# Unused bf16 products ahead of TensorE's steps in the last four experts of a mixture-of-experts layer

## The chip, the core and the metric

The kernel runs on one core of a Trainium2 chip. The metric is device time in microseconds (us) of one execution. A core has engines that run side by side, each in its own order: TensorE (PE in the profile, with PEld for its weight loads), VectorE (DVE), ScalarE (ACT), GpSimd (POOL) and SyncE (SP), which here issues the transfers from HBM.

## The reference, cut to what matters

One layer of a decoder: a token mixer of two attentions, a norm, and then a mixture of experts over 256 tokens of width 1024 in fp32. A router picks 4 of 32 experts for each token. For each expert, on the rows `xb` that go to it:

```
gu = xb @ w_gu[e] + b_gu[e]                 # 1024 -> 2048
gate = minimum(gu[:, :1024], 7); up = clip(gu[:, 1024:], -7, 7)
act = (up + 1) * gate * sigmoid(1.702 * gate)
y[token] += weight * (act @ w_down[e] + b_down[e])   # 1024 -> 1024
```

The result is the norm of `alpha * h + y`. The weights of all 32 experts, six pieces of 2 MB an expert, are read from HBM once.

## The kernel before, in words

The mixer takes the first part of the span. Then a loop over `j` from 0 to 31 (line 1142) takes the experts one after the other, in an order that `SCHED` fixes by their rank in number of tokens; it gives each a block of 64 rows (two blocks for two of them) or, for those with few tokens, of 32 rows. The numbers of experts here are places in this order. Expert 27 has 64 rows and experts 28 to 31 have 32 each.

The weights of an expert come in six transfers, called chunks here: chunks 0 to 3 are `w_gu` and chunks 4 and 5 are `w_down`, of 2 MB each. They land in a ring of ten slots, in the order of the list `SEQUENCE`; `fill` (line 434) issues the next one on SP's queue when a slot comes free. In the last expert chunks 4 and 5 are issued as four halves of 1 MB, in the order (4, first), (5, first), (4, second), (5, second).

TensorE's work is cut into steps. `expert_in` (line 877) makes one half of `gu` from two chunks; `expert_out` (line 935) makes `dn` from chunks 4 and 5. With 32 rows a step multiplies two pieces of the contraction by 512 columns into four strips of the array, so that there are two steps to a chunk; with 64 rows there are four steps to a chunk. An fp32 product is two instructions in the trace, so that a chunk is 16 instructions. For the last expert `expert_out` works on 256 columns at a time: first all four steps of the left half, then all four of the right half.

`step` (line 164) runs a step and then what is due after it: `later(n, f)` puts f behind the n-th step from there. In this way the transposes of `gu` (tile `gup`, line 910, through the matrix of sums where there are 32 rows), the turning of the gates (`ogp`, line 840), the gathering of rows (`xgp`, line 855), the last norm's rows spread over the partitions (`lnp`, line 816) and the addition of `dn` to the sum (`y`, line 960) stand between the steps. `gup`, `ogp`, `xgp` and `lnp` share one PSUM tag, `tp`, with two buffers.

For `j` the loop does the first half of `gu` (`way_in(j, 0)`), `way_out(j - 1)`, and the second half of `gu`; for `j` = 31 both halves stand ahead of `way_out(30)`. Behind the loop stands a branch for experts that have more tokens than rows (line 1164; its body isn't run here), then `way_out(31)`, the norm and the output.

At its very start the kernel multiplies the bf16 tile `ones`, 128x128, by itself 31 times (tile `warm`, line 157). The result isn't used.

Of the kernel before, what the change touches and what calls it, by code (L numbers as in the profile page):

```python
# [7 lines left out]
F32 = mybir.dt.float32  # L8
# [11 lines left out]
NE = 32  # L20
# [47 lines left out]
def layer(ctx: ExitStack, tc: tile.TileContext, x_tok, x_t, wmix, b_gate, lam, subln, ln, lnc, w_r, b_r, *rest):  # L68
    nc = tc.nc
# [33 lines left out]
    ones = cp.tile([128, 128], BF)  # L103
# [15 lines left out]
    ps1 = ps1s.enter_context(tc.tile_pool(name="ps1", bufs=1, space=PSUM))  # L119
# [44 lines left out]
    def step(f):  # L164
        f()
        for d in waiting:
            d[0] -= 1
        due = [d for d in waiting if d[0] <= 0]
        waiting[:] = [d for d in waiting if d[0] > 0]
        for d in due:  # L170
            d[1]()
# [648 lines left out]
    def norm_spread():  # L820
        w = chunks["norm"]
        for i in range(4):
            later(3 + 3 * i, lambda i=i: nc.scalar.copy(w[:, i * 512:i * 512 + 512], spread(1, i)))

    def onehot(rank, oh):
        for t in range(2):
            nc.vector.tensor_scalar(oh[:, t], cst[:, C_IO:C_IO + oh.shape[2]], rank[t], None, op0=OP.is_equal)
# [19 lines left out]
    def gather(oh, n):  # L847
        xgs.append(xgs.pop(0))
        xg = xgs[-1][0].tile([128, 8, 128], F32, tag=xgs[-1][1], name="xg")

        def half(k):
            p = ps1.tile([128, 4, 128], F32, tag="tp", name="xgp", bufs=2)
            for i in range(4):
                for t in range(2):
                    nc.tensor.matmul(p[:, i, 0:n], x1[:, t, (k + i) * 128:(k + i) * 128 + 128], oh[:, t, 0:n],  # L855
                                     start=t == 0, stop=t == 1)
            assert len(rows_done) in (0, 4)
            if rows_done:
                nc.vector.tensor_copy(xg[:, k:k + 4, 0:n], p[:, :, 0:n])  # L859
                return  # L860

            for i in range(4):
                g, b = lncol[:, 0, k + i:k + i + 1], lncol[:, 1, k + i:k + i + 1]
                if i % 2:
                    nc.scalar.activation(xg[:, k + i, 0:n], p[:, i, 0:n], AF.Identity, bias=b, scale=g)  # L865
                else:
                    nc.vector.tensor_scalar(xg[:, k + i, 0:n], p[:, i, 0:n], g, b, op0=OP.mult, op1=OP.add)
        later(1, lambda: half(0))
        later(2, lambda: half(4))
        return xg  # L870

    def bias_of(w):
        bias = cp.tile([128, 16], F32, tag="bgu", name="bgu", bufs=3)
        nc.gpsimd.tensor_copy(bias, w[:, 4096:SLOT])  # L874
        return bias

    def expert_in(ws_, xg, at_, w, n, done, between=None):


        g = ps1.tile([128, 512], F32, tag="s", name="gu", bufs=2)  # L880
        m = 64 // w

        def some(k):
            for i in range(2 * m):
                e, u = divmod(i, 2)
                o = ((k + e) % 4 * 2 + u) * 512
                nc.tensor.matmul(g[i * w:i * w + w, :], xg[:, k + e, at_:at_ + w], ws_(2 * n + k // 4)[:, o:o + 512],  # L887
                                 start=k == 0, stop=k + m == 8)
        for k in range(0, 8, m):
            step(lambda: some(k))  # L890
            if done and (k + m) % 4 == 0:
                done(2 * n + k // 4)
            if between and 0 < k < 5:
                between(k + 3)
        return g
# [25 lines left out]
    def back(d, ogT, cs, ended=None, delay=2):  # L921

        dn = wk.tile([128, 512], F32, tag="gt", name="ds_", bufs=3)
        nc.scalar.copy(dn[:, cs], d)  # L924

        def add():
            for t in range(2):
                for n in range(2):
                    rs = slice(n * 64, n * 64 + 64)
                    add_to_y(ogT[rs, t], dn[rs, cs], t, n, cs)  # L930
                if ended:
                    ended(t, cs)
        later(delay, add)

    def expert_out(ws_, act, ogT, w, done, last=False):


        m = 64 // w

        def some(d, k, cs):  # L940
            q = slice(cs.start // 256, cs.stop // 256)
            for i in range(2 * m):
                n, e = divmod(i, m)
                of = ws_(4 + (k + e) // 4).rearrange("p (q k n c) -> p k n q c", q=2, k=4, n=2)
                nc.tensor.matmul(d[i * w:i * w + w, :].rearrange("p (q c) -> p q c", c=256), act[:, k + e],  # L945
                                 of[:, (k + e) % 4, n, q], start=k == 0, stop=k + m == 8, skip_group_check=True)

        for cs in [slice(0, 256), slice(256, 512)] if last else [slice(0, 512)]:
            d = ps1.tile([128, cs.stop - cs.start], F32, tag="s", name="dn", bufs=2)
            for k in range(0, 8, m):  # L950
                step(lambda: some(d, k, cs))
                if done and cs.stop == 512 and (k + m) % 4 == 0:
                    done(4 + k // 4)
            back(d, ogT, cs, last_norm if last else None, 0 if cs.start else 2)
# [8 lines left out]
    def cols(a, k, j):  # L963
        return [a[:, k + t, j:j + 1] for t in range(2)]

    def rank(j, b):

        if b == 0:
            return cols(rgs, 0, j)
        r = cp.tile([128, 2], F32, tag="rk", name="rk", bufs=4)  # L970
        nc.vector.tensor_scalar(r, rgs[:, 0:2, j], 64.0 * b, None, op0=OP.subtract)
        return [r[:, t:t + 1] for t in range(2)]
# [60 lines left out]
    def scale_rows():  # L1033

        def part(c, i):
            rows_done.append((c, i))
            p = spread(0, 2 * i + c)
            for t in range(2):
                z = x1[:, t, c * 512:c * 512 + 512]
                nc.vector.tensor_tensor(z, z, p, op=(OP.mult, OP.add)[i])  # L1040
        for c in range(2):
            for i in range(2):
                later(4 + 4 * c + 2 * i, lambda c=c, i=i: part(c, i))
# [32 lines left out]
    def prepare(j):  # L1076

        for b in range(len(SCHED[j][1])):
            if (j, b) not in place:
                oh = wk0.tile([128, 2, 128], F32, tag="oh", name="oh")  # L1080
                n, found = 0, {}
                for jb in blocks[blocks.index((j, b)):]:
                    w = SCHED[jb[0]][1][jb[1]]
                    if n + w > 128:
                        break
                    onehot(rank(*jb), oh[:, :, n:n + w])
                    found[jb] = n
                    n += w
                xg = gather(oh, n)
                place.update({jb: (xg, k) for jb, k in found.items()})  # L1090

    def residual(n):

        bdn = wk.tile([NE, 512], F32, tag="gt", name="bdn", bufs=3)
        nc.scalar.dma_start(bdn, b_down[:, n * 512:n * 512 + 512])
        aid = wk0.tile([128, 128], F32, tag="oh", name="aid")
        nc.vector.tensor_scalar(aid, ident, ALPHA, None, op0=OP.mult)
        for t in range(2):
            later(2 + t, lambda t=t: add_to_y(aid, x1[:, t, n * 512:n * 512 + 512], t, n))
        for t in range(2):  # L1100
            later(6 + t, lambda t=t: add_to_y(rgT[:, 2 + t], bdn, t, n))
# [16 lines left out]
    def done(j, c):  # L1118
        consumed.add((j, c))
        while order_left and order_left[0] in consumed:  # L1120
            order_left.pop(0)
            fill()
# [13 lines left out]
    def way_out(j):  # L1136
        ns = SCHED[j][1]
        for b, w in enumerate(ns):
            expert_out(lambda c: chunks[j, c], acts[j][b], ogTs[j][b], w,
                       (lambda c: done(j, c)) if b == len(ns) - 1 else None, j == NE - 1)  # L1140

    for j, (_, ns) in enumerate(SCHED):
        if j in RESIDUAL:
            residual(RESIDUAL.index(j))
        if j == NE - 3:
            norm_spread()
        if j + 1 < NE:
            prepare(j + 1)
        if j == RESIDUAL[0] - 1:
            scale_rows()  # L1150
        way_in(j, 0)
        if j == NE - 1:
            way_in(j, 1)
        if j:
            way_out(j - 1)
        ogTs[j] = [weighted(rank(j, b), cols(rgs, 2, j), w) for b, w in enumerate(ns)]
        if j < NE - 1:
            way_in(j, 1)
# [50 lines left out]
    for t, c in ((0, 1), (1, 0), (1, 1)):  # L1209
# [3 lines left out]
        for u in range(1 + t * c):  # L1213
            n = 512 >> t * c
# [112 lines left out]
```

## Time and profile before

| | us |
|---|---|
| median of 3 runs | 1212.2 |
| the three runs | 1212.0, 1212.2, 1214.49 |
| the profiled execution's own time | 1211.38 |
| its span, first to last instruction | 1209.6 |
| TensorE busy in the span | 1112.9 |
| mean granted TensorE clock | 0.958 of full speed |

The span is what the trace shows. The profiled execution's own time is 1.8 us longer than its span, and 0.8 us less than the median of the runs. Times below count from the start of the span.

### The profile page before, as it was taken

The page shows a single profiled execution, that of the slowest core. Times are in us where ns is not written, and L with a number is a line of the kernel's source. Part 1 is how long each engine was busy: PE and PEld are TensorE (multiplying, and loading weights), DVE is VectorE, ACT ScalarE, POOL GpSimd, SP SyncE. Part 2 cuts the span into 40 slices and gives each one's busy share as a digit, 9 for nine tenths or more (in the row PEclk, how much of TensorE's full clock was granted, in tenths as well). Part 3 has the DMA queues.
Part 4 walks back from the last instruction along what each step waited for, and adds up shares of the span by engine and source line. Part 5 has one row for each costly group of instructions (what it writes and reads, how often), then busy time and mean ns, then how long its engine had stood idle before and what let it go on. Part 6 is the DMA issues. An engine that isn't in the chain of part 4 may idle for free. (4 is left out here: it accounts for less than half of the span.)

```text
span 1209.6 us, 15833 instructions
## 1 busy us (share of the span) xinstructions
PE 1112.9 (92%) x6294; PEld 543.1 (45%) x6294; DVE 374.0 (31%) x974; ACT 264.7 (22%) x559; POOL 63.6 (5%) x142
## 2 busy tenths in 40 slices
PE   9999999999999999999999988988888887988765
PEld 7888768885443344343334423332323232322222
DVE  5677675675232212212211211221211121111103
ACT  5555564543111112111101110110010100001100
POOL 1233220001000000000000000000000000000001
PEclk9999999999999999999999998999989999978887
DMA  9574348577999999999999999999999999999994
GB/s 354 203 266 147 134 167 338 209 279 299 395 427 427 426 428 427 427 427 424 428 420 428 427 429 425 428 428 426 429 427 426 429 427 428 428 428 428 427 427 184
DMA packets 34350, 451.49 MB, mean 373 GB/s; under 512 B 4097, under 2 KB 5281, under 8 KB 6881
## 3 DMA queue, kind: packets, MB, share of 16 engines
q1 hardware_dynamic: 34176, 450.31, 89.4%
q8 instruction: 51, 0.84, 0.3%
q14 instruction: 27, 0.21, 0.0%
q10 hardware_dynamic: 96, 0.13, 0.0%
HBM read 449.37 MB, written 1.05 MB: 372 GB/s over the span
## 5 line engine op out<-in xcount | busy, mean ns | idle before, releaser
L887 PE MATMUL gu<-w,xg 128*64 128x512 f32 (+1 forms) x2176 | 420.2, 625 | 53.6 <-DMA w<-in_wg_dram 53.3
L887 PEld LDWEIGHTS gu<-w,xg 128*64 128x64 f32 (+1 forms) x2176 | 111.4, 127 | 280.3 <-issue 249.9
L945 PE MATMUL dn<-w,act 128*64 128x512 f32 (+2 forms) x1120 | 212.2, 621 | 24.8 <-DMA w<-in_wd_dram 23.8
L913 DVE TENSOR_TENSOR h<-gup,bgu 128x512 f32<-128x512 f32 (+1 forms) x68 | 39.6, 582 | 468.1 <-PE gup L908 256.6
L945 PEld LDWEIGHTS dn<-w,act 128*64 128x64 f32 (+1 forms) x1120 | 59.4, 129 | 149.8 <-issue 121.5
L152 DVE TENSOR_TENSOR wl<-w,wh 128x512 fp32r<-128x512 f32 x140 | 99.1, 730 | 61.1 <-ACT wh L151 60.4
L232 PE MATMUL acc<-wh,xh 128*128 128x512 f32 x256 | 105.0, 410 | 1.3 <-ACT wh L151 1.3
L233 PE MATMUL acc<-wl,xh 128*128 128x512 f32 x256 | 101.8, 398 | 1.4 <-POOL wl L152 0.8
L234 PE MATMUL acc<-wh,xl 128*128 128x512 f32 x256 | 101.1, 395 | 0.0
L151 ACT CAST wh<-w 128x512 fp32r<-128x512 f32 x148 | 89.0, 621 | 52.0 <-PE acc L234 39.9
L901 ACT COPY gt<-gu 128x512 f32<-128x512 f32 x68 | 39.9, 587 | 248.9 <-PE gu L887 248.7
L915 ACT ACTIVATE act<-h 128x256 f32<-128x256 f32 (+1 forms) x68 | 25.4, 374 | 256.0 <-DVE h L914 256.0
L855 PEld LDWEIGHTS xgp<-oh,x 128*128 128x128 f32 x448 | 56.4, 205 | 14.1 <-issue 12.1
L855 PE MATMUL xgp<-oh,x 128*128 128x128 f32 (+1 forms) x448 | 60.7, 293 | 0.6 <-ACT xg L865 0.6
L859 DVE COPY xg<-xgp 128x384 f32<-128x384 f32 (+1 forms) x18 | 11.1, 615 | 144.8 <-PE xgp L855 144.6
L232 PEld LDWEIGHTS acc<-wh,xh 128*128 128x128 f32 x256 | 49.8, 195 | 12.4 <-ACT wh L151 2.4
L233 PEld LDWEIGHTS acc<-wl,xh 128*128 128x128 f32 x256 | 49.7, 194 | 12.1 <-DVE wl L152 2.1
L234 PEld LDWEIGHTS acc<-wh,xl 128*128 128x128 f32 x256 | 49.6, 194 | 9.3
L874 POOL COPY bgu<-w 128x16 f32<-128x16 f32 x32 | 6.9, 215 | 856.9 <-DMA w<-in_wg_dram 768.1
L841 ACT COPY ogT<-ogp 128x256 f32<-128x256 f32 x34 | 12.7, 372 | 135.6 <-PE ogp L840 135.6
L910 PEld LDWEIGHTS gup<-cst,gt 128*128 128x128 f32 x224 | 29.5, 206 | 26.1 <-issue 24.4
L910 PE MATMUL gup<-cst,gt 128*128 128x64 f32 x224 | 33.5, 297 | 0.0
(333 smaller groups left out, 841.2 us busy)
## 6 DMA issues: line engine op xcount, KB each, us to landing
w<-in_wg_dram SPq DMA_DIRECT2D x98, 2048.0 KB, 34.7
w<-in_wd_dram SPq DMA_DIRECT2D x64, 2048.0 KB, 38.7
w<-in_wg_dram SPq DMA_DIRECT2D x32, 2056.0 KB, 34.4
w<-in_wmix_dram SPq DMA_DIRECT2D x15, 2048.0 KB, 8.8
w<-in_wd_dram SPq DMA_DIRECT2D x4, 1024.0 KB, 33.4
xw<-in_x_t_dram SPq DMA_DIRECT2D x4, 384.0 KB, 4.6
xw<-in_x_t_dram SPq DMA_DIRECT2D x2, 768.0 KB, 8.1
bgate<-in_b_gate_dram SPq DMA_DIRECT2D x2, 512.0 KB, 6.6
```

The source lines that it names most:

```text
L151: nc.scalar.copy(h, src)
L152: engine.tensor_tensor(l, src, h.bitcast(F32), op=OP.subtract)
L232: nc.tensor.matmul(o, h, hl[0][:, cs], start=first, stop=False)
L233: nc.tensor.matmul(o, h, hl[1][:, cs], start=False, stop=False)
L234: nc.tensor.matmul(o, l, hl[0][:, cs], start=False, stop=last)
L855: nc.tensor.matmul(p[:, i, 0:n], x1[:, t, (k + i) * 128:(k + i) * 128 + 128], oh[:, t, 0:n], start=t == 0, stop=t == 1)
L887: nc.tensor.matmul(g[i * w:i * w + w, :], xg[:, k + e, at_:at_ + w], ws_(2 * n + k // 4)[:, o:o + 512], start=k == 0, stop=k + m == 8)
L901: nc.scalar.copy(gt, g)
L910: nc.tensor.matmul(to, of, cst[:, C_SUM:C_SUM + 64], start=True, stop=True)
L913: nc.vector.tensor_tensor(h, p, bias[:, :, :, None].to_broadcast([128, 4, 2, w]), op=OP.add)
L915: nc.scalar.activation(a, h[:, :, 0], AF.Sigmoid, scale=1.702)
L945: nc.tensor.matmul(d[i * w:i * w + w, :].rearrange("p (q c) -> p q c", c=256), act[:, k + e], of[:, (k + e) % 4, n, q], start=k == 0, stop ...
```

## The change

A function `idle(n)` issues n products of the bf16 tile `ones`, 128x128, by itself into a PSUM tile under the tag `tp`, which nothing reads. It does so only once the list `idling` holds something, which is from `j` = 28 on. It is called ahead of every step: with n = 9 in `expert_in` and `expert_out`, and in the last expert's `expert_out` with n = 5 for the left half and not at all for the right half.

```
+    idling = []
+
+    def idle(n):
+
+        if idling:
+            p = ps1.tile([128, 128], F32, tag="tp", name="idle", bufs=2)
+            for _ in range(n):
+                nc.tensor.matmul(p, ones, ones, start=True, stop=True)
+
     def bias_of(w):
...
         for k in range(0, 8, m):
+            idle(9)
             step(lambda: some(k))
...
             for k in range(0, 8, m):
+                if not last:
+                    idle(9)
+                elif not cs.start:
+                    idle(5)
                 step(lambda: some(d, k, cs))
...
+        if j == NE - 4:
+            idling.append(j)
         if j == RESIDUAL[0] - 1:
             scale_rows()
         way_in(j, 0)
```

## Rows read from the trace of the kernel before

**Rows 1.** The page: span, and granted clock and traffic in 40 slices

```profile
span 1209.6 us, 15833 instructions
...
PEclk9999999999999999999999998999989999978887
DMA  9574348577999999999999999999999999999994
```

**Rows 2.** The chain that ended last, in order of time: start, us, what

```profile
1192.93 2.80 PE dn L945 x48
1195.72 1.11 PE y L960 x8
1196.83 1.04 PE dn L945 x16
```

**Rows 3.** Stretches of 5 us at the end: busy by engine, granted clock, DMA share, GB/s

```profile
1155.00:1160.00 5.00, 3.29 (x24) 0.81 (x20) 0.00 (x0) 0.96 (x2) 0.00 (x0) 1.00 0.99 420
1160.00:1165.00 5.00, 2.96 (x24) 1.47 (x24) 1.37 (x5) 0.31 (x1) 0.20 (x1) 1.00 0.99 421
1165.00:1170.00 5.00, 3.55 (x16) 0.59 (x16) 0.00 (x0) 0.59 (x1) 0.00 (x0) 0.66 1.03 436
1170.00:1175.00 5.00, 3.08 (x28) 1.59 (x32) 1.37 (x5) 0.31 (x1) 0.00 (x0) 1.00 1.01 429
1175.00:1180.00 5.00, 3.09 (x20) 0.53 (x21) 0.00 (x0) 0.59 (x1) 0.00 (x0) 0.55 1.00 424
1180.00:1185.00 5.00, 5.00 (x24) 2.08 (x23) 0.00 (x0) 0.00 (x0) 0.00 (x0) 0.50 0.98 411
1185.00:1190.00 5.00, 4.24 (x20) 1.08 (x22) 1.89 (x7) 0.90 (x2) 0.00 (x0) 0.59 0.76 313
1190.00:1195.00 5.00, 4.18 (x50) 1.94 (x52) 0.00 (x0) 0.37 (x1) 0.00 (x0) 1.00 0.29 116
```

**Rows 4.** Shorter stretches, where the weights' traffic ends (columns as in rows 3)

```profile
1194.00:1194.50 0.50, 0.50 (x16) 0.30 (x12) 0.00 (x0) 0.00 (x0) 0.00 (x0) 1.00 0.08 33
1194.50:1195.00 0.50, 0.50 (x16) 0.33 (x12) 0.00 (x0) 0.00 (x0) 0.00 (x0) 1.00 0.00 0
```

**Rows 5.** TensorE in order of time: start, us, what, count, idle before and its releaser

```profile
1080.87 3.68 PE L945 MATMUL dn<-w,act 128*64 128x512 f32 x8 [1.89 <-DMA w<-in_wd_dram]
...
1086.39 7.22 PE L945 MATMUL dn<-w,act 128*64 128x512 f32 x24
...
1170.08 1.92 PE L887 MATMUL gu<-w,xg 128*32 128x512 f32 x16 [1.43 <-DMA w<-in_wg_dram]
1171.94 1.10 PE L910 MATMUL gup<-cst,gt 128*128 128x64 f32 x8
1174.88 3.09 PE L887 MATMUL gu<-w,xg 128*32 128x512 f32 x16 [1.84 <-DMA w<-in_wg_dram]
1179.88 3.64 PE L945 MATMUL dn<-w,act 128*32 128x512 f32 x16 [1.91 <-DMA w<-in_wd_dram]
1183.45 1.97 PE L910 MATMUL gup<-cst,gt 128*128 128x64 f32 x8
1185.35 3.64 PE L945 MATMUL dn<-w,act 128*32 128x512 f32 x16
1189.75 1.99 PE L960 MATMUL y<-ds__7348,ogT 64*128 64x512 f32 x8 [0.76 <-ACT ds__7348 L924]
1191.67 0.44 PE L840 MATMUL ogp<-cst,og 128*128 128x128 f32 x2
1192.93 2.80 PE L945 MATMUL dn<-w,act 128*32 128x256 f32 x48 [0.82 <-ACTq L1164]
```

**Rows 6.** SyncE's queue in order of time: start, us, the issues

```profile
1150.56 14.84 SPq L450 DMA_DIRECT2D w<-in_wd_dram  x4
```

**Rows 7.** The page, DMA issues: count, KB each, median us from issue to landing

```profile
w<-in_wd_dram SPq DMA_DIRECT2D x64, 2048.0 KB, 38.7
```

**Rows 8.** TensorE at the start of the kernel (columns as in rows 5)

```profile
1.05 3.49 PE L157 MATMUL warm<-ones 128*128 128x128 bf16 x31 [1.05 <-DVE ones L105]
```

## The prediction

> **What bounds the kernel now.** I begin with the page [rows 1]. From the middle of the span on, the slices of the line DMA stand at 9 and more: the weights come in without a pause. The line of TensorE's clock is 9 nearly throughout and falls to 7 and 8 in the last fifth, where the four changed experts lie. So the first question is which of the two, the stream of weights or TensorE at a low clock, sets the end.
>
> The chain that ended last [rows 2] has nothing of the stream. In the traced tail it is TensorE's: 48 instructions of the last expert's `dn` from 1192.93, eight of `y`, the last 16 of `dn` from 1196.83, and from there the last `y`, the norm and the output. In the short stretches [rows 4] the weights' traffic is still 33 GB/s up to 1194.5 and nothing after it. The last 16 instructions need the last half chunk, so they could start at about 1194.5 at the earliest, and did 2.3 us later. That is all that a faster TensorE can win in the tail: whatever the change does to the clock before, the end moves forward by at most 2.3 us, which is 0.19% of the time. About 0.2%, or 2.4 us, is also what a measurement of this kernel can tell from no change.
>
> Then I read where those 2.3 us were lost. In the timeline of TensorE [rows 5] chunks start at 1170.08, 1174.88 and 1179.88, each after a wait for a DMA: a chunk lands every 4.9 us, and up to here TensorE is early. From 1179.88 it waits no more for weights: `dn` takes 3.64 us, `gup` 1.97, the next `dn` 3.64, where the same 16 instructions took 1.92 at 1170.08 and `gup` 1.10. [...] At full clock those three would have left TensorE waiting again for the chunk that lands at 1179.88 + 4.9 = 1184.8.
>
> What TensorE did before the clock fell: in 1160 to 1165 it was busy 2.96 of 5 us and in the next 5 us the mean is 0.66; in 1170 to 1175 it was busy 3.08, and then 0.55 follows. The waits ahead of the chunks there are 1.43 to 1.91 us [rows 5]. What it did before the clock rose: 5.00 and 4.24 of 5 us, without a wait for weights, and from 1190 on it is 1.00 [rows 3].
>
> **The change part by part.**
>
> *How many products.* Experts 28 to 31 have 8 steps of `gu` each, 32 in all; `way_out(27)`, which also lies behind the switch, has 8 steps with its 64 rows; `way_out` of 28 to 30 has 4 each, 12. That is 52 x 9 = 468, and 4 x 5 = 20 in the last expert: 488 products.
>
> *What one costs.* The trace has the same product at the start [rows 8]: 31 in 3.49 us, (3.49 - 0.31) / 30 = 0.106 us from one to the next, 0.31 being the length of one by itself. I take this as the upper end. Work in these experts shrinks from 3.64 to 1.92 between half and full clock [rows 5]; the same factor 0.53 gives 0.056 as the lower end. No row has bf16 products with a weight load each at full clock late in the kernel; for full clock I take 0.07, nearer to the lower end because 128 columns have the length of a quarter of a 512-column pass, and above it because every product brings its own load. Nine then cost 0.63 us, five 0.35; at half clock 0.95 and 0.53.
>
> [...]
>
> *Where it costs nothing.* In a chunk with two steps there are 18 products, 1.26 us at full clock. A light chunk is then 1.92 + 1.26 = 3.2 of 4.9 us, one with `gup` 4.3 us. This stands in the wait for the next chunk, since nothing that the products read is late. Only `way_out(27)` has no room. Its 32 instructions took 3.68 + 7.22 us [rows 5], and 72 products add 5 us there. TensorE falls some 4 us behind and makes it up in the light chunks of experts 28 to 30, with 1.7 us of room each. A slot then comes free up to 4 us late; but a chunk is issued 38.7 us before it lands [rows 7], so the stream keeps its queue full. The last four issues, at 1150.56 and the 14.84 us after it [rows 6], stand 30 us ahead of the end of the traffic. If this cover were gone, the stream would lose those 4 us. I cost it at nothing.
>
> *The shared PSUM tag.* `idle` takes a buffer of `tp`, so it waits until the reader of the tile two back is done. Between two fillers there is a step of 0.9 us or more at full clock, and in the tail only `gup` and `ogp` share the tag, which are read within that. Zero at best. At worst, at the chunk with `gup`, it waits for one read of some 0.5 us, taken from the room of a light chunk.
>
> *The tail, with full clock.* From the landing at 1184.8: a step, nine products, a step, 1.92 + 0.63 = 2.55, so `dn` ends at 1187.3. The work before it (from 1179.88: 1.92 + 1.10 + 18 products 1.26 = 4.3, to 1184.2) just fits. Before, `dn` began at 1185.35 and ended at 1188.99. The wait for ScalarE's copy, 0.76, stays: `y` at 1188.1. From `y` to the last expert's first step the distance was 1192.93 - 1189.75 = 3.18: 1191.3, which is 1.65 earlier. Here the change takes back: 20 products ahead of the left half stand on the path, 20 x 0.07 = 1.4 us. The rest, 2.80 + 1.11, is as it was at full clock. So the last 16 instructions start 1.65 - 1.4 = 0.25 us earlier, 1196.6. With 0.056 it is 0.7 us earlier; with 0.106 for the products it is 0.8 us later. The sum: 1211.38 - 0.25 = 1211.1 us against the profiled execution's own time.
>
> The runs' median is 0.8 above that execution, and one run is 3 us above. TensorE's clock near the end is what I take to differ between them, as it is the one thing in the tail with two levels; the fillers would even that out. I put the forecast halfway between 1211.1 and 1212.2 - 0.25: **1211.5 us**.
>
> **The rivals.**
>
> *A, the clock holds (forecast): 1211.5 us.* For it: with fillers the light chunks are 3.2 of 4.9 us with shorter waits, and those with `gup` 4.3, where the falls followed stretches of 2.96 and 3.08 of 5 us. 1155 to 1160, with 3.29 of 5, was followed by full clock [rows 3]. Against it: 3.2 of 4.9 isn't far from what fell.
>
> *B, the clock doesn't hold, and the fillers are paid at half clock on the path: slower.* Its place is the two chunks from 1179.88. At half clock 18 products ahead of the second `dn` and nine within it add 27 x 0.106 = 2.85 us to a path that already had no wait, and the 20 in the last expert 1.4 more at full clock: 4.25 us later, 1211.38 + 4.25 = **1215.6**. If the last expert too runs at half clock, 64 instructions of 3.8 us double and it is near 1220. It decides once the clock is at half for more than about 6 of the 9 us from 1179.88. For it: the clock stayed at half for over 9 us there, through 5.00 busy of 5 [rows 3], so being busy doesn't lift it at once. Against it: dense bf16 products are what the kernel issues at its very start, and they close the waits from which the falls came.
>
> *C, a short fall: no change.* Half clock in one of the two last `dn` of expert 30 alone costs 3.64 - 1.92 = 1.7 us [rows 5] on the path: 1211.1 + 1.7 = **1212.8**. For it: the falls before lasted from one stretch to three [rows 3].
>
> *D, the tail reaches the stream: faster.* If the products cost less than 0.056, or hide behind weight loads, the tail ends at its bound, 1211.38 - 2.3 = **1209.1**; and if the ordinary execution of before is the later one, 1212.2, the difference is up to 3 us. Against it: 20 products stand on the path.
>
> *E, the code does nothing,* as the clock is full anyway in most executions: the 20 products alone, + 1.4: **1212.8** to 1213.6, no change.
>
> **How the numbers follow.** A 0.52, B 0.13, C 0.13, D 0.12, E 0.10. Slower by over 0.2% is B (0.13); faster by over 0.2% is D (0.12) and 0.02 of A where the runs before are late ones (0.14 in all); the rest, 0.73, is within 0.2%. The range holds A, C and E and reaches to D's 1209.1, of which it leaves out a part, and towards B: 1209.8 to 1215.0.
>
> **What would show it.** If A is right: granted clock near 1.00 in 1155 to 1195, `dn` of 16 instructions interleaved with fillers at 1179.9 and 1184.8, each after a wait for a DMA; a gap of 0.06 to 0.08 us between fillers; the last 16 of `dn` between 1194.5 and 1196.8; DMA at its full rate to the same 1194.5. Wrong if the clock is near 0.5 after 1180 (B), if traffic ends later than 1194.5 or the stream has pauses after expert 27 (slots late), or if `idle` stands waiting for DVE or ACT.

## The result, and the profile after

| | us |
|---|---|
| after, median of 5 runs | 1219.03 (1218.08 to 1219.34) |
| before, median of 5 runs | 1212.0 (1211.54 to 1214.49) |
| ratio after to before | 1.0051, 95% interval 1.004 to 1.0062 |
| profiled execution after: own time, span | 1218.12, 1216.3 |

The change makes the kernel slower by 0.5%. The forecast was 1211.5 us with a range of 1209.8 to 1215.0; the measured time lies above it.

The page of the kernel after, with the lines that answer to [rows 1]:

```profile
span 1216.3 us, 16807 instructions
...
PEclk9999999999999999999999989999997999999997
DMA  9574348578999999999999999999999999999992
```

TensorE's clock no longer falls in the last fifth, but for the very last slice; the single 7 lies well before the changed experts. The weights come in as before. The change does to the clock what it could do, and the kernel is slower none the less. The stretches of the kernel after, which answer to [rows 3] (busy PE, PEld, DVE, ACT and POOL, granted clock, DMA share, GB/s):

```profile
1080.00:1110.00 30.00, 29.42 (x261) 14.15 (x265) 3.26 (x12) 2.75 (x6) 0.20 (x1) 1.00 1.01 429
1110.00:1140.00 30.00, 28.23 (x271) 14.16 (x267) 3.26 (x12) 4.99 (x10) 0.20 (x1) 1.00 1.01 426
1140.00:1155.00 15.00, 12.05 (x110) 5.17 (x110) 1.89 (x7) 0.90 (x2) 0.00 (x0) 1.00 1.01 426
1155.00:1190.00 35.00, 27.75 (x274) 12.95 (x272) 4.63 (x17) 3.64 (x8) 0.20 (x1) 1.00 0.96 405
1190.00:1195.00 5.00, 0.57 (x4) 0.20 (x2) 0.00 (x0) 0.37 (x1) 0.00 (x0) 0.78 0.36 147
1195.00:1200.00 5.00, 4.75 (x40) 2.00 (x41) 0.00 (x0) 0.00 (x0) 0.00 (x0) 0.53 0.01 3
```

Up to 1190 the clock is 1.00. From 1190 to 1195 TensorE is busy for 0.57 us only, and then the clock is 0.53. What it waits for stands in its timeline, which answers to [rows 5]:

```profile
1179.88 1.06 PE L955 MATMUL dn<-w,act 128*32 128x512 f32 x8 [1.61 <-DMA w<-in_wd_dram]
1180.87 0.68 PE L879 MATMUL idle<-ones 128*128 128x128 bf16 x9
1181.48 1.06 PE L955 MATMUL dn<-w,act 128*32 128x512 f32 x8
...
1184.78 1.07 PE L955 MATMUL dn<-w,act 128*32 128x512 f32 x8 [0.70 <-DMA w<-in_wd_dram]
...
1188.21 1.99 PE L974 MATMUL y<-ds__7868,ogT 64*128 64x512 f32 x8 [0.76 <-ACT ds__7868 L934]
1190.13 0.44 PE L840 MATMUL ogp<-cst,og 128*128 128x128 f32 x2
1195.25 0.69 PE L879 MATMUL idle<-ones 128*128 128x128 bf16 x5 [4.68 <-PEq L1180]
1195.87 1.08 PE L955 MATMUL dn<-w,act 128*32 128x256 f32 x8
...
1200.35 1.50 PE L955 MATMUL dn<-w,act 128*32 128x256 f32 x24
...
1202.89 1.07 PE L955 MATMUL dn<-w,act 128*32 128x256 f32 x16
```

Until 1190.5 TensorE is ahead of the kernel before: `y` starts at 1188.21 instead of 1189.75. Then it stands still for 4.68 us, released by its own sequencer at line 1180. That is the branch around the experts with too many tokens, whose body isn't run here; before, 0.82 us passed at this place, ended by ScalarE [rows 5]. The instructions of that line show the branch itself. First that of before (line 1164 there), then that of after (count, and duration in ns):

```profile
L1164 PEldq COMPARE_BRANCH  x1: 445/445/445, 1190.5 to 1190.5; - x1
```

```profile
L1180 PEldq COMPARE_BRANCH  x1: 5938/5938/5938, 1189.0 to 1189.0; - x1
```

The same branch takes 5.94 us in place of 0.45. The time goes as follows, in the profiled executions. The last expert starts 1195.25 - 1192.93 = 2.32 us later: 1.54 won before the branch and 3.86 lost at it. From there to its last 16 instructions 1202.89 - 1195.25 = 7.64 us pass instead of 3.83, through the 20 products and through the clock of 0.53 that follows the standstill. From there to the end of the span it is 13.4 instead of 12.8, for a reason given at the end. Together that is 2.32 + 3.81 + 0.6 = 6.7, the whole difference of the spans.

### The profile page after: what moved, and what is told of

It reads as the page before. It is cut to its first block, busy times and chain, and to the rows that moved or that the text cites. A ratio compares the mean times of both kernels' runs of the same rounds, so it can differ in the third digit from the quotient of the medians.

```text
span 1216.3 us, 16807 instructions
## 1 busy us (share of the span) xinstructions
PE 1128.6 (93%) x6782; PEld 561.9 (46%) x6782; DVE 374.9 (31%) x974; ACT 264.1 (22%) x559; POOL 62.6 (5%) x142
## 5 line engine op out<-in xcount | busy, mean ns | idle before, releaser
L896 PE MATMUL gu<-w,xg 128*64 128x512 f32 (+1 forms) x2176 | 413.4, 608 | 41.4 <-DMA w<-in_wg_dram 41.3
L955 PE MATMUL dn<-w,act 128*64 128x512 f32 (+2 forms) x1120 | 207.7, 597 | 22.8 <-DMA w<-in_wd_dram 22.6
L896 PEld LDWEIGHTS gu<-w,xg 128*64 128x64 f32 (+1 forms) x2176 | 108.4, 126 | 252.3 <-issue 219.3
L955 PEld LDWEIGHTS dn<-w,act 128*64 128x64 f32 (+1 forms) x1120 | 56.3, 126 | 132.2 <-issue 101.6
L879 PEld LDWEIGHTS <-ones 128*128 128x128 bf16 x488 | 29.0, 100 | 38.3 <-issue 33.0
L879 PE MATMUL idle<-ones 128*128 128x128 bf16 x488 | 37.6, 223 | 4.7 <-PEq L1180 4.7
```

Of the source, the lines that this page charges most:

```text
L879: nc.tensor.matmul(p, ones, ones, start=True, stop=True)
```

## The experiments

Why does a branch that skips the same work take 5.5 us more? `idle` is called wherever `expert_in` and `expert_out` are called, and the branch's body calls them too. There are 24 steps in it (two times eight of `gu` and eight of `dn`, with 64 rows), so 216 products, each a load and a product: 432 more TensorE instructions that are never run but stand between the branch and its target. **Theory S**: the jump is slow because of their number. **Theory T**: it is slow because TensorE comes to it earlier, while the weights still come in. The first four runs have the products in some of these places and not in others.

**e1**, the change without the products in the body:

```
             xg = gather(oh, 64)
             drain()
+            idling.clear()
...
             expert_out(w12.__getitem__, act, ogT, 64, None)
             drain()
+            idling.append(NE)
```

> The changed kernel with no unused products in the body of the branch that isn't run; all others stay. Theory S (the jump over the body is slow because the body grew by 432 TensorE instructions): the wait behind the branch shrinks from 4.68 us to about 0.8 us, the clock stays full, and the time is that of the forecast, 1211.1 us, against 1218.1 in the profiled execution of the change. Theory T (the jump is slow because TensorE, now earlier, reaches it while the weights still come in): the wait stays, TensorE goes on at about 1195.2 us, and the time stays near 1218.

Measured: 1212.94 us (before in the same session 1211.82; ratio 1.0009, interval 1.0000 to 1.0018). The branch and TensorE's timeline behind it in e1:

```profile
L1180 PEldq COMPARE_BRANCH  x1: 1878/1878/1878, 1189.2 to 1189.2; - x1
```

```profile
1188.46 1.99 PE L974 MATMUL y<-ds__7868,ogT 64*128 64x512 f32 x8 [0.76 <-ACT ds__7868 L934]
1190.38 0.44 PE L840 MATMUL ogp<-cst,og 128*128 128x128 f32 x2
1191.64 0.44 PE L879 MATMUL idle<-ones 128*128 128x128 bf16 x5 [0.81 <-ACTq L1180]
1192.01 0.64 PE L955 MATMUL dn<-w,act 128*32 128x256 f32 x8
...
1197.41 1.07 PE L955 MATMUL dn<-w,act 128*32 128x256 f32 x16
```

TensorE comes to the branch about as early as with the change, at 1189.2, while the weights still come in (162 GB/s from 1190 to 1195), and waits 0.81 us, again for ScalarE. That is the wait that S gave, and T by itself is refuted. S's time is missed: the profiled execution has 1213.56 us and not 1211.1, for reasons given under "Why the prediction was wrong". The branch takes 1.88 us here, against 0.45 in the kernel before, but it ends ahead of ScalarE, so that none of it shows. The 6.1 us between the medians of the change and of e1 (with 1212.0 and 1211.82 for before beside them) are the price of instructions that never run.

**e2**, the other way round: the kernel before with the products in the body alone (`idling` is filled ahead of the body and cleared behind it, and not at `j` = 28).

> The kernel before with the unused products only in the body of the branch, where none is ever run. Theory S: TensorE works as before up to the branch, the branch takes 5.9 us instead of 0.45 us from about 1190.5, the last expert starts at about 1196.7 instead of 1192.9, and the time is 1211.4 + 3.8 = 1215.2 us, up to 1217 if the clock falls in the wait. Theory T: nothing that is run has changed, so 1211.4 to 1212.2 us.

Measured: 1215.39 us, ratio 1.003 (1.002 to 1.0041), where TensorE runs not one instruction more than before. That is S's time. The trace is of the fastest of the eight executions, 1213.18 us; the branch is long here too:

```profile
L1178 PEldq COMPARE_BRANCH  x1: 4914/4914/4914, 1189.5 to 1189.5; - x1
```

```profile
1188.81 3.79 PE L974 MATMUL y<-ds__7348,ogT 64*128 64x512 f32 x8 [0.74 <-ACT ds__7348 L934]
1192.52 0.44 PE L840 MATMUL ogp<-cst,og 128*128 128x128 f32 x2
1194.77 2.80 PE L955 MATMUL dn<-w,act 128*32 128x256 f32 x48 [1.81 <-PEq L1178]
```

The sequencer takes the branch at 1189.5, while `y` and `ogp` are still at work, so that they hide three of the 4.91 us and only 1.81 show. So in this execution the last expert starts at 1194.77 and not at S's 1196.7; what the slower executions did isn't on record. In the change the work ahead of the branch runs at full clock and is shorter (`y` takes 1.99 us, here 3.79), and it hides less of it.

**e3**, the change without the products of the last expert (`elif not cs.start: idle(5)` taken out):

> The changed kernel without the 20 products of the last expert, body of the branch as in the change. Both theories: the wait of 4.7 us stays. The four groups of five took 0.62 to 0.65 us each, partly at half clock, 0.38 at full clock, together 2.3 us: 1218.1 - 2.3 = 1215.8 us. If the products instead lift the clock after the wait, less is won, and it stays above 1216.5.

Measured: 1216.5 us, ratio 1.0039 (1.0025 to 1.0052); the profiled execution has 1215.7, where 1215.8 was expected.

```profile
1194.72 4.75 PE L955 MATMUL dn<-w,act 128*32 128x256 f32 x48 [4.78 <-PEq L1178]
```

The wait stays, as both theories say. The 20 products cost 2.5 us between the medians. Without them the 48 instructions take 4.75 us in place of 2.80 [rows 5], and the granted clock behind the wait, from 1195 to 1200, is 0.63.

**e4**, both together: no products in the body and none in the last expert, the other 468 as in the change.

> No products in the body of the branch and none in the last expert; the 468 others stay. Theory S: the 0.8 us wait, the last expert's products from 1191.3 us at full clock without 20 products on the path: 1211.1 - 1.5 = 1209.6 us, with the last weights' landing as the bound at 1209.1. Theory T: the wait lasts to about 1195.2, near 1215.

Measured: 1210.80 us against 1211.82, ratio 0.999 (0.9981 to 0.9999).

```profile
1191.70 2.80 PE L955 MATMUL dn<-w,act 128*32 128x256 f32 x48 [0.82 <-ACTq L1178]
1194.47 1.13 PE L972 MATMUL y<-ds__8085,ogT 64*128 64x256 f32 x8
1195.53 1.07 PE L955 MATMUL dn<-w,act 128*32 128x256 f32 x16
```

The last 16 instructions start 1.2 us earlier than before, by this timeline and that of the kernel before (1196.76 there). Of the 2.3 us that the bound leaves, e4 wins 1.0 by its median, and the interval ends just below no change. S's 1209.6 isn't reached: the last expert starts 0.4 us later than S had it, as in e1, and the norm takes 0.6 us longer, for the reason given at the end.

**e5 to e7**: is it a cliff, or does the wait grow with the body? The kernel of e4 with 2, 4 and 6 products ahead of each step in the body:

```
         if idling:
+            n = idling[0] if idling[0] < 10 else n
...
-            idling.clear()
+            idling[:] = [2]        # 4, 6
```

> The kernel of e4 (468 products in the loop, none in the last expert) with 2 unused products ahead of each of the 24 steps in the body of the branch, 96 more TensorE instructions in it. If the jump has a cliff (its target is either among what TensorE has already fetched or not), the wait is either 0.82 us as in e4 or some 4.8 as in e3, and it steps once between none and nine. If the wait grows with the length of the body, it is 0.82 + 2 x 0.44 = 1.7 us.

> The same with 4 products ahead of each step in the body, 192 more instructions. Cliff: 0.82 or 4.8 us. Growing with the length: 0.82 + 4 x 0.44 = 2.6 us.

> The same with 6 products ahead of each step in the body, 288 more instructions. Cliff: 4.8 us, most likely, as nine are 432 instructions. Growing with the length: 0.82 + 6 x 0.44 = 3.5 us.

One execution each, so without an interval: 1210.85, 1217.65 and 1217.37 us (the kernel before has 1210.55 to 1213.32 in the same session). The branches of e5, e6 and e7:

```profile
L1179 PEldq COMPARE_BRANCH  x1: 1785/1785/1785, 1189.1 to 1189.1; - x1
```

```profile
L1179 PEldq COMPARE_BRANCH  x1: 6018/6018/6018, 1189.4 to 1189.4; - x1
```

```profile
L1179 PEldq COMPARE_BRANCH  x1: 5128/5128/5128, 1190.3 to 1190.3; - x1
```

And the last expert's first steps behind them:

```profile
1191.47 1.93 PE L956 MATMUL dn<-w,act 128*32 128x256 f32 x32 [0.82 <-ACTq L1179]
```

```profile
1195.76 5.35 PE L956 MATMUL dn<-w,act 128*32 128x256 f32 x48 [4.71 <-PEq L1179]
```

```profile
1195.70 5.35 PE L956 MATMUL dn<-w,act 128*32 128x256 f32 x48 [3.82 <-PEq L1179]
```

TensorE's waits are 0.82, 4.71 and 3.82 us. It is a cliff: 96 more instructions cost nothing, 192 cost the whole wait, and 288 and 432 no more than that. The 3.82 of e7 by itself would also fit a wait that grows (3.5), the 4.71 of e6 doesn't (2.6). In e7 `y` starts 0.8 us later than in e6 and so hides more of the branch, which ends at 1195.4 in both.

The body of before has 78 fp32 operations for TensorE by its code. Of these 68 are products (16 `xgp`, 32 `gu`, 16 `dn` and 4 `y`), each of them two loads and two products in the trace; 10 are transposes (2 `ogp` and, with 64 rows, 8 `gup`), each one load and one product. That is 292 instructions. So the step lies between some 388 and 484 instructions to jump over. Why it lies there no run shows.

The traces also have packets of 16 KB on an instruction queue. First its packets in the kernel before, then in the changed one, which runs 976 TensorE instructions more, then those of the changed one from 1192 to 1193.5, within the branch (count, MB, share of the DMA engines):

```profile
q8 instruction: 51, 0.84, 0.3%
```

```profile
q8 instruction: 55, 0.90, 0.3%
```

```profile
q8 instruction: 1, 0.02, 4.3%
```

In each of the five traces with a long branch (the change, e2, e3, e6 and e7) such a packet starts 2.4 to 3.5 us after the branch does, takes 1.0 us, and the branch ends 1.5 us after it has landed. In the five with a short one (before, e1, e4, e5 and e8) no packet starts within the branch: it ends 1.4 us after the landing of one that was under way or there before TensorE came to it. In the change the branch goes from 1189.00 to 1194.94 and the packet from 1192.39 to 1193.41; in the kernel before the branch goes from 1190.49 to 1190.93 and the packet ahead of it from 1188.45 to 1189.54. That the long branch waits for its packet is inferred from these times alone: what a packet holds, and what asks for it, the traces don't show. Where the step lies for another branch wasn't tried.

**e8**, on the other half of the change: four products in place of nine, else as e4.

> The kernel of e4 with 4 products in place of 9 ahead of each step. If it is the closed waits that keep the clock up, four (0.3 us instead of 0.68 a step) leave waits of 2.4 us in the light chunks, the clock falls in them as before, and the time is 1211.4 to 1212.2 us, as before. If any products between the steps are enough, the clock stays at 1.00 up to 1190 and the time is that of e4, 1210.8 us.

Measured: 1210.62 us against 1211.99, ratio 0.9991 (0.9982 to 1.0000), the time of e4. Stretches of e8:

```profile
1100.00:1120.00 20.00, 16.70 (x136) 7.05 (x128) 3.26 (x12) 2.96 (x6) 0.00 (x0) 0.91 1.01 426
1120.00:1140.00 20.00, 18.63 (x130) 8.06 (x130) 1.37 (x5) 2.93 (x6) 0.20 (x1) 0.83 1.01 427
1140.00:1160.00 20.00, 15.36 (x118) 5.36 (x114) 1.89 (x7) 1.85 (x4) 0.08 (x1) 0.91 1.01 428
1160.00:1180.00 20.00, 13.16 (x120) 4.92 (x112) 2.74 (x10) 1.79 (x4) 0.11 (x1) 1.00 1.00 423
1180.00:1200.00 20.00, 13.82 (x142) 6.52 (x134) 6.17 (x20) 2.64 (x6) 1.27 (x3) 0.97 0.50 208
```

Neither expectation holds as it stands. With four products the clock does fall at times between 1100 and 1160, as the first said, but in the profiled execution it is full from 1160 until TensorE's work is done (the 0.97 is from after that), and the time is that of the second. The short branch takes 2.42 us here and shows a little, as TensorE waits 1.01 us for its own sequencer:

```profile
1190.83 2.80 PE L955 MATMUL dn<-w,act 128*32 128x256 f32 x48 [1.01 <-PEq L1178]
```

## Why the prediction was wrong

*The clock (rival A) was right* for the change: the stretch from 1080 to 1190 has 1.00, and the two last `dn` of expert 30 start at 1179.88 and 1184.78 after waits for a DMA, as they were to. Nine products take 0.61 us (1180.87 to 1181.48), where the sum had 0.63. At the clock of 1.00 each of the four steps of those two `dn` takes 1.06 or 1.07 us; before, at 0.50, two steps took 3.64 [rows 3, rows 5]. No `idle` waits for VectorE or ScalarE. It doesn't hold in every execution: e7 has the same nine products ahead of each step, and after a wait of 2.09 us its clock fell all the same, as rival C had it:

```profile
1180.00:1185.00 5.00, 4.61 (x29) 1.68 (x29) 0.00 (x0) 0.00 (x0) 0.00 (x0) 0.66 0.99 415
```

*Expert 27* cost the stream nothing, as forecast: DMA share 1.01 to 1155. But its lag was 0.9 us (1094.45 against 1093.54 at the end of its steps) and not 4. The 3.68 + 7.22 us that the sum added the products to were run at a granted clock of 0.50 in the kernel before (1080 to 1090), and at full clock the steps are shorter: 1.08 us each in the change, at 1.00, where the first two had taken 3.68.

*Rival B*, whose numbers (1215.6, and near 1220 with the last expert at half clock) are the nearest to the measured one, is refuted as a mechanism: nothing was paid at half clock ahead of the branch. The last expert did run in part at half clock (0.53 from 1195 to 1200), but after the standstill.

*The step that failed* is "From `y` to the last expert's first step the distance was 1192.93 - 1189.75 = 3.18: 1191.3". It took the place between them, with its branch, for unchanged. It was 7.04 us (1188.21 to 1195.25). The part before it, *how many products*, counted the 488 that are run and left out the 216 in the body of the branch, which calls the same two functions. The text on the kernel before named the branch and said that its body isn't run; that the body's length could matter was not asked. With the body left as it was, e1 has 1191.64 for that step against 1191.3, and 0.26 us of this is that its weights landed later in its span.

*A term mis-sized:* the 20 products of the last expert. The sum had 1.4 us. At full clock they cost 5.77 - 3.83 = 1.94 us (from the first to the last 16 instructions, e1 and e4), and 2.1 between the medians of e1 and e4. Five products take 0.37 to 0.39 us, where the sum had 0.35. The rest is that a step of `dn` behind them takes 0.57 us, where six of them in a row took 2.80, 0.47 each [rows 5]. So e1, the change without its hidden part, isn't at the sum's 1211.1 either. In its profiled execution, 1213.56, the last 16 instructions start 0.8 us later than the sum had them (the 20 products and the later weights), the norm takes 0.6 us longer, and the time outside the span is 2.7 us in place of 1.8. By the medians e1 is 1.1 us above the kernel before, with an interval that begins at no change.

*An argument that the runs don't bear out:* that the executions of before differ by TensorE's clock near the end, and that the products would even this out, which moved the forecast from 1211.1 to 1211.5. The eleven executions of e4 still lie between 1209.09 and 1212.57, and its profiled one has a granted clock of 1.00 from 1080 on. What makes executions differ stays open.

*The bound held.* No version went below 1209.1 by its median, and in e5 the last expert waits 0.46 us for a DMA: there TensorE has caught up with the stream.

*Left open:* why the jump takes nearly 6 us when the packet takes 1.0. What passes in the 2.4 to 3.5 us ahead of it and the 1.5 us behind it, the traces don't show. It isn't a wait for the end of the weights' traffic: in all five traces the packet has landed before that end, and the branch ends 0.1 to 0.7 us after the one but always 1.5 us after the other. Whether the traffic makes the jump longer, as a part of T would have it, is untested, since no run has the long jump with an idle stream. Nor does a run show what TensorE has fetched when it comes to the branch, by which e5's expectation explains a cliff; what is shown is the step in the time.

## What to carry to other kernels

When a helper gets more instructions, count every place that calls it, those in branches that don't run too: here the 216 products that never run cost 6.1 us, while the 468 in the loop, which are run, cost nothing that can be told (e4). A branch on the path near the end should have its target close behind it (here it took 0.45 to 2.42 us over some 292 to 388 TensorE instructions and 4.9 to 6.0 over 484 and more), or work that hides it, as `y` did in part in e2. And before paying for a faster engine in a stretch, ask what the tail could win at most: here it was 0.2%.

## What the runs showed of the hardware that was not expected

- The cost of this kernel's skipped body has a step: TensorE's branch takes 0.45 to 2.42 us over some 292 to 388 TensorE instructions, and 4.9 to 6.0 us over some 484 to 724. Only TensorE's part of the body grew; ScalarE's branch at the same line takes 45 ns before and after.
- A long branch ends 1.5 us after a 16 KB packet has landed on an instruction queue, in all five traces that have one.
- After a standstill of 4.7 us in the change the granted clock is 0.53 from 1195 to 1200; in e1, where the wait is 0.81, it is 1.00. The last expert's steps take 1.9 us longer (7.64 - 5.77).
- In the norm at the end VectorE's first product with the bias (512 columns) takes 0.75 us in some executions and 1.85 in others, when it starts within 0.05 us of a GpSimd product on another part of the same tile. In the change:

```profile
1208.42 1.85 DVE L1233 SCALAR_TENSOR_TENSOR x<-x,mv,w 128x512 f32<-128x512 f32 x1
```

and in e5:

```profile
1201.83 0.75 DVE L1234 SCALAR_TENSOR_TENSOR x<-x,mv,w 128x512 f32<-128x512 f32 x1
1201.88 1.82 POOL L1224 TENSOR_TENSOR x<-x,w 128x512 f32<-128x512 f32 x1
```

  Where VectorE has 1.85, GpSimd has 1.26, and the end comes 0.6 us later. This is the 0.6 us in the sum of the result. It is seen with and without the long branch (e4 has 1.85, e2 0.75), and what decides it wasn't tried.
